# Low parts of the retention weights: accumulating transfers in place of VectorE subtractions, and an earlier latent statistic

## The chip, the cores and the metric

One core of one Trainium2 chip runs the whole program. The metric is the device time of one execution in microseconds (us). The kernel before was timed three times: 1770.57, 1771.42 and 1773.42 us, median 1771.42 us.

## What is computed

Two layers of a diffusion backbone work on 512 latent tokens and 256 context tokens of width 1024. Layer 0 is windowed attention with a SwiGLU feed-forward part; layer 1 is bidirectional retention with a second SwiGLU. The change lies where layer 0 hands over to layer 1 and in layer 1's retention, cut here to what matters:

```python
def bidir_retention(h_x, h_c, w_qkvg, decay_logit, gn_gain, w_o, need_ctx_out):
    q_x, k_x, v_x, g_x = jnp.split(h_x @ w_qkvg, [qk, 2 * qk, 2 * qk + RET_VWIDTH], axis=-1)
    ...
    k_c, v_c = jnp.split(h_c @ w_qkvg[:, qk:2 * qk + RET_VWIDTH], [qk], axis=-1)
    ...
    ox_f, _ = retention_chunked(q_x, k_x, v_x, log_g[0], state_f)
    ox_b, _ = retention_chunked(flip(q_x), flip(k_x), flip(v_x), log_g[1], state_b)
    out_x = gated_out(ox_f + flip(ox_b), g_x)

# around it, for each layer
h_x = modulate(rms_norm(x, norm1_g[i]), mx[0], mx[1])
h_c = modulate(rms_norm(y_ctx, norm1_g[i]), mc[0], mc[1])
```

There are 4 retention heads, each with 256 query and key columns and 512 value and gate columns. All is float32.

## The kernel before

**Two parts of every operand.** The TensorE (PE) works on a rounded float32 type. So each float32 operand is split into a high part (the rounded value) and a low part (the operand minus the high part), and each product is three matmuls: high x high, low x high, high x low (`mm3`, `product_q`, `product_v`). The second of them already needs the weight's low part.

**A weight on its way.** Weights lie in DRAM as a row of chunks `wst[i]`, 128 x 1024 each (512 KB). `chunk(i)` (line 1155) starts the load on SP's queue into a raw buffer: `wraw`, of which there are 2, or `wx`, of which there are 4 and which the retention's scores use too. `w_parts` (line 126) hands out one of four pairs of buffers `whi`, `wlo`, two in the pool `rp` and two in `qp`, in turn. `split` (line 164) writes `whi` by a cast on ACT and `wlo` by a subtraction on VectorE (DVE). `split_chunk` (line 1160) does this for q, k, v and g weights and keeps its last instruction in `last_split`, on which some orders of instructions are hung; `next_w` (line 136) loads, casts and subtracts in one for the output weights. A pair of buffers is free again when PE has done its last product with it, a raw buffer when its last reader is done.

**The products are of Strassen's kind.** The tokens and the rows of the weights are cut in halves, and one of the weight operands is a sum or difference of chunks, made by DVE in place in the raw buffers. For the query and key of a head (lines 1352 to 1358), q12 = q22 - q12 (L1353), k11 = q12 + k11 (L1354), w2 is the split of this k11, k21 = k21 - k11 (L1356), k11 = q22 - k11 (L1357), and w1, w3, w22, w4 are the splits of k11, q12, q22, k21. For gate and value it is L1388, L1389 and L1394 (w2, w3, w4), and after the scores L1454 (w1).

**The order in a head** (loop at line 1310): key weights k11, k21 and their products with latent and context tokens; the five query products w2, w1, w3, w22, w4; rotation of the query; the second half of the value weights, b21 (in head 0 this comes before the keys); w2, w3, w4 of gate and value; six rounds of scores and outputs (lines 1414 to 1448); w1 and w22 of the gate; norm and gate; the first value weights of the next head (`first_weights_v`); the output projection (`out_tile`), 2 tiles per weight chunk. In the last head the output is done in two halves, between them the first weights of the next feed-forward part (`first_weights`, line 1546), which keep their own cast and subtraction.

**Queues.** SP issues the raw loads in order. In this part nobody uses POOL's queue, but for some adds of squares in the last head. Each engine works in order; the order on each engine is set by a scheduler when the program is built, except in stretches marked as written by hand, which are not touched here.

**The hand-over.** `output(prev, True)` (line 1132) makes the last output tiles of layer 0: 8 latent tiles, then 8 context tiles. `square_and_stats` (line 1035) is called after each. For a latent tile it adds its square into a running sum (ACT and DVE). For a context tile it squares it on ACT and adds it up over partitions with a matmul by ones into a PSUM bank of the pair `pj`; after the second context tile it switches ACT's table (`ln_exp_turn`) and makes the latent statistic (`rms(0)`), whose bank is the other one of the pair.

Of the kernel before, what the change touches and what calls it, by code (L numbers as in the profile page):

```python
# [11 lines left out]
AF = mybir.ActivationFunctionType  # L12
# [4 lines left out]
KT = D // P  # L17
SX = 512
SC = 256
# [30 lines left out]
def dit_kernel(ctx, tc, xT, cT, crow, small, consts, masks, tabs0, tabs1, jtab, adaQ, adaN, adaT, wst, out):  # L50
    nc = tc.nc
    mult, add, sub = ALU.mult, ALU.add, ALU.subtract
# [9 lines left out]
    def T(pool, cols, tag, bufs, dt=F32):  # L62
        return pool.tile([P, cols], dt, tag=tag, bufs=bufs, name=tag)

    def pj(n=512):
        return T(psJ, 512, "pj", 2)[:, :n]
# [6 lines left out]
    ones = cp.tile([P, P], F32, name="ones_sb")  # L73
# [17 lines left out]
    def after(ins, others):  # L91
        for o in others:
            tc.add_manual_dep(ins.ins, o.ins.name, order, reason="table set turn")

    def ln_exp_turn():
        pre = nc.scalar.preload_act_table_set("natural_log_exp_and_others")
        after(pre, turn["silu"])
        turn.update(pre=pre, lnexp=[], silu=[])
# [19 lines left out]
    wpos, wsel, ring = [0], [0], []  # L118

    def w_raw(pool=None, bufs=2):  # L120
        raw = T(pool or rp, 1024, "wraw", bufs)
        nc.sync.dma_start(raw, wst[wpos[0]])
        wpos[0] += 1
        return raw

    def w_parts(pool, own=2):

        bufs = own
        if ring:
            pool, bufs = ring[wsel[0] % len(ring)], 2  # L130
        elif wsel[0] % (2 + own) < 2:
            pool, bufs = rp, 2
        wsel[0] += 1
        return T(pool, 1024, "whi", bufs, F32R), T(pool, 1024, "wlo", bufs, F32R)

    def next_w(pool, own=2, raw=None):

        raw = raw or w_raw()
        hi, lo = w_parts(pool, own)
        nc.scalar.copy(hi, raw)  # L140
        nc.vector.tensor_tensor(lo, raw, hi, op=sub)  # L141
        return hi, lo

    def mm3(o, w, x, first, last):

# [18 lines left out]
    def split(t, hi, lo):  # L164
        nc.scalar.copy(hi, t)  # L165
        return nc.vector.tensor_tensor(lo, t, hi, op=sub)  # L166


    def load_stream(s, engines=(nc.sync, nc.sync)):
        res = []  # L170
        if s == 0:
            for k in range(KT):
                t = T(rp, 512, "res", 12)
                eng = engines[k % 2] if k < 4 else nc.sync
                ins = eng.dma_start(t, xT[:, k, :])
                if eng is nc.scalar:
                    turn["lnexp"].append(ins)
                res.append(t)
        else:
            for k in range(0, KT, 2):  # L180
                t = T(rp, 512, "res", 12)
                nc.sync.dma_start(t.rearrange("p (a n) -> p a n", a=2), cT[:, k:k + 2, :])
                res += [t[:, 0:SC], t[:, SC:2 * SC]]
        return res

    def t_sq(n):
        return T(rp, 512, "sq", 2)[:, :n]
# [7 lines left out]
    def neg_half_rstd(y, z, tot, count, behind=()):  # L195

        after(lnexp(y, tot, AF.Ln, scale=1.0 / count, bias=eps), behind)
        lnexp(y, y, AF.Exp, scale=-0.5)
        nc.scalar.activation(z, y, AF.Square, scale=0.5 / math.sqrt(count))
        nc.vector.scalar_tensor_tensor(z, tot, count * EPS, z, add, mult)  # L200
        nc.vector.scalar_tensor_tensor(y, z, -0.75, y, add, mult)
# [3 lines left out]
    def add_square(s, k, t, c=slice(None), eng=nc.vector, tmp=t_sq, fresh=True):  # L205

        if k == 0:
            if fresh:
                ssq[s] = t_y(s)
            return nc.scalar.activation(ssq[s][:, c], t[:, c], AF.Square)  # L210
        sq = tmp(NTOK[s])[:, c]
        ins = nc.scalar.activation(sq, t[:, c], AF.Square)
        eng.tensor_tensor(ssq[s][:, c], ssq[s][:, c], sq, op=add)
        return ins

    def rms(s, c=slice(None), bank=pj, behind=()):
        y = ssq[s][:, c]
        n = y.shape[1]
        tot = bank()[:, :n]
        after(nc.tensor.matmul(tot, ones, y, start=True, stop=True), behind)  # L220
        neg_half_rstd(y, t_sq(n), tot, D)
# [150 lines left out]
    raw = []  # L372
# [444 lines left out]
    for g in range(NKV):  # L817
        final = g == NKV - 1
        for i, (s, b) in enumerate(context + latent if final else latent + context):
# [7 lines left out]
            if final and i > 1:  # L827
                d = early[i - 2]
# [3 lines left out]
        if g == 2:  # L832
            split_o(2)
            wo0 = wpos[0]
            cres = load_stream(1)
# [11 lines left out]
    for d4 in range(0, KT, 4):  # L847
        wpos[0] = wo0 + max(d4, 2)
        w = [next_w(wo_p) if d > 1 else wo_w[d] for d in range(d4, d4 + 4)]
# [183 lines left out]
    ctx_sum = []  # L1033

    def square_and_stats(s, d, t):
        if s == 0:
            add_square(s, d, t)
            return
        if d == 0:
            ctx_sum.append(pj(SC))  # L1040
        sq = t_sq(SC)
        nc.scalar.activation(sq, t, AF.Square)
        nc.tensor.matmul(ctx_sum[0], ones, sq, start=d == 0, stop=d == KT - 1, skip_group_check=True)
        if d == 1:
            ln_exp_turn()
            rms(0)

    def spare_w():

        raw, w = w_raw(), (T(fp, 1024, "wraw", 1, F32R), T(fp, 1024, "adaw", 1, F32R))  # L1050
        split(raw, *w)
        return w
# [95 lines left out]
    qp = R.enter_context(tc.tile_pool(name="qp", bufs=1, reuse_waits="tile"))  # L1148
# [4 lines left out]
    chunk_base = wpos[0]  # L1153

    def chunk(i, own=False):
        raw = T(qw, 1024, "wx", 4) if own else T(rp, 1024, "wraw", 2)
        nc.sync.dma_start(raw, wst[i])
        return raw

    def split_chunk(raw):  # L1160
        w = w_parts(qp)
        last_split[0] = split(raw, *w)
        return w

    last_split, hm = [None], []

# [67 lines left out]
    def product_v(os, a, w, first, tiles=(0, 1), by_k=False):  # L1234

        for t, k in ((t, k) for k in range(4) for t in tiles) if by_k else ((t, k) for t in tiles for k in range(4)):
            tok = slice(t * P, t * P + P)
            whi, wlo = (p[:, k % 2 * 512:k % 2 * 512 + 512] for p in w[k // 2])
            xhi, xlo = (x[:, tok] for x in a(k))
            for i, (p, r) in enumerate(((xhi, whi), (xhi, wlo), (xlo, whi))):  # L1240
                ins = nc.tensor.matmul(os[t], p, r, start=first and k + i == 0, stop=k == 3 and i == 2,  # L1241
                                       skip_group_check=by_k or not first)
        return ins
# [42 lines left out]
        return t[:, 0:512], t[:, 512:1024]  # L1286

    def first_weights_v(hd):
        return [split_chunk(chunk(chunk_base + 16 * hd + 4 + i)) for i in range(2)]

    def values_first(w, by_k=False):

# [17 lines left out]
    for hd in range(RH):  # L1310
        bq = chunk_base + 16 * hd
        bv, bg = bq + 4, bq + 8

        def other_values():

            b21 = [split_chunk(chunk(bv + i)) for i in (2, 3)]
            Xv = [W4("X"), W4("X")]
            product_v(Xv, quarter_of("12"), b21, True)
            for t in range(2):
                nc.vector.tensor_tensor(vt[t], vt[t], Xv[t], op=add)  # L1320
            c = cv if hd else context_values(b11)
            product_v(c, context_half(1), b21, False)
            vt.extend((T(rp, 512, "y0", 1), T(qp, 512, "vc", 1)))
            for t in range(2):
                nc.scalar.copy(vt[4 + t], c[t])

        if hd == 0:
            other_values()
        k11, k21 = split_chunk(chunk(bq)), split_chunk(chunk(bq + 1))
        if hd == 0:  # L1330
            sums = token_sums(hm, 0, T(qp, 64, "sh2", 1), h_sum, [normed])
            dx, dcx = strips(0, [sums])
# [19 lines left out]
        q12, q22, k11, k21 = chunk(bq + 2, True), chunk(bq + 3, True), chunk(bq), chunk(bq + 1)  # L1352
# [2 lines left out]
        w2 = split_chunk(k11)  # L1355
        nc.vector.tensor_tensor(k21, k21, k11, op=sub)  # L1356
        nc.vector.tensor_tensor(k11, q22, k11, op=sub)  # L1357
        w1, w3, w22, w4 = (split_chunk(r) for r in (k11, q12, q22, k21))
        while strip_sums:
            after(strip_sums.pop(), [last_split[0]])  # L1360
        Y2 = W4("Y")
# [20 lines left out]
        g12, w2, w4 = [], [], []  # L1382
# [8 lines left out]
        w3 = [split_chunk(g) for g in g12]  # L1391
# [59 lines left out]
        w1 = []  # L1451
        for i in range(2):
            g, v = chunk(bg + i), chunk(bv + i)
            nc.vector.tensor_tensor(g, g, v, op=sub)  # L1454
            w1.append(split_chunk(g))
        w22 = [split_chunk(chunk(bg + 2 + i)) for i in range(2)]
        Zg = [W4("Z"), W4("Z")]
        last = hd == RH - 1
        product_v(Zg, quarter_of(1), w1, True)
# [10 lines left out]
        r, z = mv[:, 8:12], mv[:, 12:16]  # L1470
# [53 lines left out]
        w = []  # L1524

        def out_tile(d, c, tags="XY"):
            while len(w) * 2 <= d:
                w.append(next_w(qp))
            oo = (W4(tags[d % 2]) if tags[d % 2] != "j" else pj())[:, c]
            for k in range(4):  # L1530
                c0 = k * 256 + (d % 2) * P
                mm3(oo, (w[d // 2][0][:, c0:c0 + P], w[d // 2][1][:, c0:c0 + P]),
                    (yt[k][0][:, c], yt[k][1][:, c]), k == 0, k == 3)
            return nc.vector.scalar_tensor_tensor(xr[d][:, c], oo, mods[1, 0][:, 2, d:d + 1], xr[d][:, c], mult, add)

        if hd < RH - 1:
            for d in range(KT):
                out_tile(d, slice(0, SX))
            continue
        w += [next_w(qp) for _ in range(4)]  # L1540
        H.close()
        hM, hW, hX = (ctx.enter_context(tc.tile_pool(name=n, bufs=1, reuse_waits="tile", side="right"))
                      for n in ("hM", "hW", "hX"))
# [141 lines left out]
    for gsz in FFN_GROUPS:  # L1685
        acts = []
        for i in range(gsz):
            if f < 2:
                acts.append(first[f])
            elif f == 2:  # L1690
                w = [next_w(fp), next_w(fp)]
# [153 lines left out]
```

## Time and profile before

| | before |
|---|---|
| median of three runs | 1771.42 us |
| the profiled execution | 1769.85 us |
| its span in the trace | 1768.1 us |
| PE clock granted | 1.00 (mean 0.999) |
| DMA engines' busy share in the retention part (890 to 1415 us) | 0.40 |
| splits of a weight chunk there | 100 (25 per head) |

"Busy" is the time in which an engine had an instruction of the program at work. PE's matmuls overlap and their ends are modelled, so PE's busy time is an upper bound. A row of groups gives line, engine, operation, output and inputs with their shapes, the count, and after the bar the busy time in us, the mean of one in ns, and the idle time before them with what ended it. A row of a timeline gives start and length in us. `PEld` is PE's weight load, `SPq` an issue on SP's queue.

### The profile page before, as it was taken

How to read it: one execution, taken by the hardware profiler on the slowest of the kernel's cores; microseconds unless marked ns; L12 is line 12 of the kernel's file. 1: busy time of each engine (PE TensorE's matmuls, PEld its weight loads, DVE VectorE, ACT ScalarE, POOL GpSimd, SP SyncE). 2: the span in 40 equal slices, each digit the busy share in tenths (PEclk: the TensorE clock that was granted, in tenths of full speed). 3: DMA queues.
4: the chain of work that ended last, by engine and by line, in shares of the span. 5: the costliest groups of instructions: out<-in, count | busy, mean ns of one | idle time of the engine just before them, and what ended most of it. 6: DMA issues, size and time to landing. Idle time of an engine off the chain costs nothing.

```text
span 1768.1 us, 27617 instructions
## 1 busy us (share of the span) xinstructions
PE 1720.8 (97%) x10876; PEld 1526.5 (86%) x10876; DVE 1355.5 (77%) x2368; ACT 843.8 (48%) x1480; POOL 131.1 (7%) x268
## 2 busy tenths in 40 slices
PE   8999999999999999999998999999999999999999
PEld 5777777789999899999987788898897889999998
DVE  6697778788779787777789858758768897777774
ACT  5576676464433334342465534534524564445442
POOL 0034434000000000000000000000000000000000
PEclk9999999999999999999999999999999999999999
DMA  9501012533243534343343534434433323233322
GB/s 352 224 15 35 25 49 72 180 114 136 74 142 119 167 119 144 121 141 116 99 133 107 161 98 138 155 96 134 153 99 116 96 86 113 90 108 108 96 84 84
DMA packets 60754, 207.73 MB, mean 117 GB/s; under 512 B 6736, under 2 KB 7120, under 8 KB 60368
## 3 DMA queue, kind: packets, MB, share of 16 engines
q1 hardware_dynamic: 53424, 180.28, 31.6%
q0 software_dynamic: 6912, 25.17, 4.6%
q8 instruction: 85, 1.39, 0.3%
q10 hardware_dynamic: 288, 0.52, 0.1%
q14 instruction: 45, 0.37, 0.1%
HBM read 203.85 MB, written 2.10 MB: 116 GB/s over the span
## 4 chain that ended last, share of the span: by engine, by line
PE 66%; DVE 17%; DMA 9%; ACT 3%; issue 3%; POOL 1%; SPq 0%; ACTq 0%; DVEq 0%; POOLq 0%
PE Y L874 13%; PE Z L874 6%; PE pj L150 6%; PE pj L149 6%; PE pj L148 6%; DMA wraw<-in_wst_dram 4%; PE X L874 3%; DVE wlo L166 3%; PE Z L1241 3%; PE Y L1230 3%; PE pT L725 2%; DMA adaw<-in_adaT_dram 2%; DVE y L274 2%; PE pO L737 2%; PE pj L1241 1%
## 5 line engine op out<-in xcount | busy, mean ns | idle before, releaser
L165 ACT CAST whi<-wraw 128x1024 fp32r<-128x1024 f32 x177 | 185.4, 1051 | 294.7 <-PE Z L150 65.3
L166 DVE TENSOR_TENSOR wlo<-wraw,whi 128x1024 fp32r<-128x1024 f32 x177 | 215.9, 1222 | 41.8 <-ACT whi L165 41.7
L874 PE MATMUL Y<-aq,whi 128*128 128x384 f32 x640 | 173.8, 335 | 0.8 <-ACT hn L1014 0.5
L256 DVE SCALAR_TENSOR_TENSOR res<-pj,mod,res 128x512 f32<-128x512 f32 (+1 forms) x112 | 81.6, 729 | 57.0 <-PE pj L150 56.4
L141 DVE TENSOR_TENSOR wlo<-wraw,whi 128x1024 fp32r<-128x1024 f32 x81 | 99.7, 1230 | 30.9 <-ACT whi L140 30.1
L874 PEld LDWEIGHTS Y<-aq,whi 128*128 128x128 f32 x640 | 116.5, 188 | 2.4 <-ACT hn L1014 1.1
L140 ACT CAST whi<-wraw 128x1024 fp32r<-128x1024 f32 x81 | 84.9, 1050 | 70.4 <-PE Z L150 22.2
L874 PE MATMUL Y<-aq,wlo 128*128 128x384 f32 x320 | 107.2, 335 | 1.9 <-DVE wlo L166 1.9
L101 ACT ACTIVATE pr<-pr,stat,qs 128x513 f32<-128x513 f32 (+2 forms) x96 | 74.3, 776 | 17.9 <-DVE stat L709 17.8
L1241 PE MATMUL Z<-whi,sA 128*128 128x512 f32 x256 | 81.0, 392 | 1.8 <-ACT whi L165 1.8
L716 POOL TENSOR_SCALAR pr<-pr,stat 128x512 f32<-128x512 f32 (+2 forms) x96 | 71.8, 761 | 77.8 <-DVE stat L713 54.2
L274 DVE CUSTOM_DVE_ANT_0 y<-adaw,crow,small_sb 128x1024 bf16<-128x1024 f32 x48 | 61.4, 1280 | 16.2 <-DMA adaw<-in_adaT_dram 16.2
L148 PE MATMUL pj<-ax,whi 128*128 128x512 f32 x176 | 68.7, 391 | 1.0 <-DVE res L256 1.0
L150 PE MATMUL pj<-ax,whi 128*128 128x512 f32 x176 | 68.6, 390 | 0.0
L149 PE MATMUL pj<-ax,wlo 128*128 128x512 f32 x176 | 68.5, 389 | 0.0
L148 PE MATMUL pj<-act,whi 128*128 128x512 f32 x168 | 66.0, 393 | 0.0
L149 PE MATMUL pj<-act,wlo 128*128 128x512 f32 x168 | 65.9, 392 | 0.0
L150 PE MATMUL pj<-act,whi 128*128 128x512 f32 x168 | 65.5, 390 | 0.0
L725 PE MATMUL pT<-const_sb,pr 128*128 128x128 f32 x352 | 57.0, 283 | 8.5 <-POOL pr L716 5.1
L874 PEld LDWEIGHTS Y<-aq,wlo 128*128 128x128 f32 x320 | 60.1, 188 | 2.5 <-DVE wlo L166 2.5
L725 PEld LDWEIGHTS pT<-const_sb,pr 128*128 128x128 f32 x352 | 38.4, 141 | 26.5 <-POOL pr L716 15.3
L874 PE MATMUL Y<-sA,whi 128*128 128x256 f32 x304 | 60.8, 283 | 0.2 <-ACT res L1647 0.2
(549 smaller groups left out, 5246.2 us busy)
## 6 DMA issues: line engine op xcount, KB each, us to landing
wraw<-in_wst_dram SPq DMA_DIRECT2D x240, 512.0 KB, 3.6
adaw<-in_adaT_dram POOLq DMA_DIRECT2D x32, 512.0 KB, 3.9
wx<-in_wst_dram SPq DMA_DIRECT2D x24, 512.0 KB, 4.8
adan<-in_adaQ_dram SPq DMA_DIRECT2D x16, 512.0 KB, 8.2
crow<-in_adaT_dram POOLq DMA_DIRECT2D x16, 512.0 KB, 4.3
adan<-in_adaN_dram SPq DMA_DIRECT2D x12, 512.0 KB, 7.6
adaw<-in_adaT_dram SPq DMA_DIRECT2D x8, 512.0 KB, 4.3
res<-in_xT_dram SPq DMA_DIRECT2D x14, 256.0 KB, 3.8
```

The costliest lines, as they stand in the source:

```text
L140: nc.scalar.copy(hi, raw)
L141: nc.vector.tensor_tensor(lo, raw, hi, op=sub)
L148: nc.tensor.matmul(o, whi, xhi, start=first, stop=False)
L149: nc.tensor.matmul(o, wlo, xhi, start=False, stop=False)
L150: return nc.tensor.matmul(o, whi, xlo, start=False, stop=last)
L165: nc.scalar.copy(hi, t)
L166: return nc.vector.tensor_tensor(lo, t, hi, op=sub)
L256: return nc.vector.scalar_tensor_tensor(res[d], o, mods[l, s][:, part, d:d + 1], res[d], mult, add)
L274: after(nc.vector.tensor_tensor_reduce(junk, w, cr[:, s * 1024:(s + 1) * 1024], 1.0, sm_t[:, C_ADAB + l * 48 + j:C_ADAB + l * 48 + j + 1], ...
L725: nc.tensor.transpose(tp[:, a * P:(a + 1) * P], self.pr[(0, 2, 1, 3)[a]][:, ki * P:(ki + 1) * P], ident)
L874: nc.tensor.matmul(o, p, r, start=first and k + i == 0, stop=k == 3 and i == 2, skip_group_check=not first)
L1241: ins = nc.tensor.matmul(os[t], p, r, start=first and k + i == 0, stop=k == 3 and i == 2, skip_group_check=by_k or not first)
```

## The change

A new function `split_dma` makes the low part without DVE: ACT writes the high part, then ACT writes minus the high part into the low part's buffer, then a transfer issued on POOL's queue adds the operand into it. The operand is read from the raw buffer, or from DRAM a second time where the chunk is used as it was loaded (`whole_chunk`), which leaves the raw buffer to its next load after the cast. All `split_chunk` calls and the retention's output weights (`next_w` with `by_dma=True`) take this way; 13 of a head's 25 read DRAM, 12 the raw buffer. `split` stays for the activations, for the other layers' weights, and for the first weights of the next feed-forward part.

In `square_and_stats`, the bank of the context's sum is now taken after `rms(0)`, and the square of a context tile follows two tiles later, the last three after the last tile.

```diff
-    def next_w(pool, own=2, raw=None):
+    def next_w(pool, own=2, raw=None, by_dma=False):
 
         raw = raw or w_raw()
-        hi, lo = w_parts(pool, own)
-        nc.scalar.copy(hi, raw)
-        nc.vector.tensor_tensor(lo, raw, hi, op=sub)
-        return hi, lo
+        w = w_parts(pool, own)
+        if by_dma:
+            split_dma(raw, *w, wst[wpos[0] - 1])
+        else:
+            split(raw, *w)
+        return w
...
+    def split_dma(t, hi, lo, src=None):
+
+        nc.scalar.copy(hi, t)
+        nc.scalar.activation(lo, hi, AF.Identity, scale=-1.0)
+        return nc.gpsimd.dma_start(lo, t if src is None else src, accum_op=add)
...
-        if d == 0:
-            ctx_sum.append(pj(SC))
-        sq = t_sq(SC)
-        nc.scalar.activation(sq, t, AF.Square)
-        nc.tensor.matmul(ctx_sum[0], ones, sq, start=d == 0, stop=d == KT - 1, skip_group_check=True)
         if d == 1:
             ln_exp_turn()
             rms(0)
+            ctx_sum.append(pj(SC))
+        for k in ((d - 2,) if 1 < d < KT - 1 else range(KT - 3, KT) if d == KT - 1 else ()):
+            sq = t_sq(SC)
+            nc.scalar.activation(sq, cres[k], AF.Square)
+            nc.tensor.matmul(ctx_sum[0], ones, sq, start=k == 0, stop=k == KT - 1, skip_group_check=True)
...
-    def split_chunk(raw):
+    def split_chunk(raw, i=None):
         w = w_parts(qp)
-        last_split[0] = split(raw, *w)
+        last_split[0] = split_dma(raw, *w, None if i is None else wst[i])
         return w
+
+    def whole_chunk(i):
+        return split_chunk(chunk(i), i)
...
-        return [split_chunk(chunk(chunk_base + 16 * hd + 4 + i)) for i in range(2)]
+        return [whole_chunk(chunk_base + 16 * hd + 4 + i) for i in range(2)]
...
-            b21 = [split_chunk(chunk(bv + i)) for i in (2, 3)]
+            b21 = [whole_chunk(bv + i) for i in (2, 3)]
...
-        k11, k21 = split_chunk(chunk(bq)), split_chunk(chunk(bq + 1))
+        k11, k21 = whole_chunk(bq), whole_chunk(bq + 1)
...
-        w1, w3, w22, w4 = (split_chunk(r) for r in (k11, q12, q22, k21))
+        w1, w3, w22, w4 = (split_chunk(r, i) for r, i in ((k11, None), (q12, None), (q22, bq + 3), (k21, None)))
...
-        w22 = [split_chunk(chunk(bg + 2 + i)) for i in range(2)]
+        w22 = [whole_chunk(bg + 2 + i) for i in range(2)]
...
-                w.append(next_w(qp))
+                w.append(next_w(qp, by_dma=True))
...
-        w += [next_w(qp) for _ in range(4)]
+        w += [next_w(qp, by_dma=True) for _ in range(4)]
```

## The prediction

> **What bounds the kernel now.** I read the page first, then the busy times by stretch, then the timelines of the stretches that lose time.
>
> ```profile
> span 1768.1 us, 27617 instructions
> ...
> PE 1720.8 (97%) x10876; PEld 1526.5 (86%) x10876; DVE 1355.5 (77%) x2368; ACT 843.8 (48%) x1480; POOL 131.1 (7%) x268
> ```
>
> TensorE (PE) is busy for 97% of the span, so no edit to another engine can give back more than PE's idle time. The change touches only the retention part, from 890 to 1415 us. In the busy times by stretch the columns are PE, PE's weight loads, DVE, ACT, POOL, PE's clock, DMA share and GB/s:
>
> ```profile
> 890.00:1415.00 525.00, 512.32 (x2791) 440.33 (x2790) 402.79 (x582) 247.44 (x385) 4.04 (x8) 1.00 0.40 125
> ...
> 930.00:940.00 10.00, 8.33 (x67) 7.93 (x66) 10.00 (x19) 5.98 (x10) 0.00 (x0) 1.00 0.16 54
> 940.00:950.00 10.00, 9.06 (x76) 8.86 (x75) 8.16 (x10) 4.13 (x8) 0.00 (x0) 1.00 0.59 203
> 950.00:960.00 10.00, 8.22 (x57) 7.26 (x55) 10.00 (x16) 5.70 (x8) 0.00 (x0) 1.00 0.39 114
> 960.00:970.00 10.00, 8.29 (x36) 6.30 (x34) 10.00 (x12) 4.10 (x6) 0.00 (x0) 1.00 0.12 34
> 970.00:980.00 10.00, 9.27 (x40) 7.45 (x41) 8.17 (x13) 5.64 (x9) 0.00 (x0) 1.00 0.74 231
> 980.00:990.00 10.00, 9.43 (x41) 7.18 (x40) 7.54 (x10) 5.32 (x7) 0.00 (x0) 1.00 0.40 116
> ```
>
> Of 525 us PE is idle for 525 - 512.32 = 12.7 us, the ceiling of any gain. The six stretches of head 0 from 930 to 990 hold 1.67 + 0.94 + 1.78 + 1.71 + 0.73 + 0.57 = 7.4 us of it, and there DVE is full (10.00 in three of them). So VectorE bounds the first head in places, and PE bounds the other three heads.
>
> **The part that goes: the subtractions.** The groups of instructions between 890 and 1415 us:
>
> ```profile
> L166 DVE TENSOR_TENSOR wlo<-wraw,whi 128x1024 fp32r<-128x1024 f32 x60 | 73.2, 1222 | 24.5 <-ACT whi L165 24.5
> L165 ACT CAST whi<-wraw 128x1024 fp32r<-128x1024 f32 x60 | 62.9, 1049 | 93.1 <-PE Y L150 52.6 <-DMA wraw<-in_wst_dram 16.0 <-DVE wraw L1454 15.0
> L166 DVE TENSOR_TENSOR wlo<-wx,whi 128x1024 fp32r<-128x1024 f32 x24 | 28.8, 1222 | 11.3 <-ACT whi L165 11.1
> L141 DVE TENSOR_TENSOR wlo<-wraw,whi 128x1024 fp32r<-128x1024 f32 x16 | 19.6, 1225 | 14.6 <-ACT whi L140 14.1
> ```
>
> All 60 + 24 + 16 = 100 go, 25 a head: 121.6 us of DVE's 402.79. In heads 1 to 3 this is worth almost nothing by itself, since PE is the bound. In head 0 I credit the whole idle time of the six rows: **-7.4 us** (bounds 0 and -7.4).
>
> **The part that comes on ACT and POOL.** 100 negations of 128x1024 on ACT, priced by the cast of the same shape at 1.05 us: 105 us, so ACT goes from 247 to 352 of 525 us. It stays under PE, but it is in order, so a negation can stand in front of a PSUM copy. POOL has 4.04 us of work in the stretch; its queue is free for 100 issues, each waiting for its negation, with nothing else behind it but the next issue and, in the last head, POOL's adds of squares. I add **+1.1 us** for one negation in front of one copy at the tail, where nothing covers it (bounds 0, and 4 x 1.05 = 4.2 for the last head's four output weights).
>
> **How late a low part becomes.** An accumulating transfer is not in this trace. The nearest rows are plain loads of the same 512 KB; the last two numbers are KB and us from issue to landing:
>
> ```profile
> wraw<-in_wst_dram SPq DMA_DIRECT2D x240, 512.0 KB, 3.6
> adaw<-in_adaT_dram POOLq DMA_DIRECT2D x32, 512.0 KB, 3.9
> adan<-in_adaQ_dram SPq DMA_DIRECT2D x16, 512.0 KB, 8.2
> ...
> q1 hardware_dynamic: 53424, 180.28, 31.6%
> ```
>
> The least is 3.9 us (POOL's own queue); the most that I allow is 8.2 us, the slowest median of a 512 KB load. The engines' time of one pass is 31.6% of 1768.1 us over 180.28 MB, which is 1.62 us for 0.524 MB. An accumulating transfer must also read what it adds to, so I take 3.9 + 1.6 = **5.5 us**. A low part then lands 1.05 + 5.5 = 6.55 us after its high part instead of 1.22 us: 5.3 us later, 100 times. Where the weight is made far ahead of its use this is hidden:
>
> ```profile
> 1031.32 1.06 ACT L165 CAST whi<-wraw 128x1024 fp32r<-128x1024 f32 x1 [4.34 <-PE Y L150]
> ...
> 1047.60 2.87 PE Y L1230 x24
> ```
>
> The first row is the cast of head 1's k11, the second (the chain) its first product, 16 us later; I price k and the output weights at nothing. The cover is those 16 us, less 7.6 for cast, negation and transfer. It is not hidden where a weight is made just in time.
>
> **Head 0, query weights.** Timeline of DVE and ACT (start, length):
>
> ```profile
> 903.14 1.22 DVE L166 TENSOR_TENSOR wlo<-wraw,whi 128x1024 fp32r<-128x1024 f32 x1
> ...
> 920.60 2.35 DVE L166 TENSOR_TENSOR wlo<-wraw,whi 128x1024 fp32r<-128x1024 f32 x2
> ...
> 935.17 1.22 DVE L1354 TENSOR_TENSOR wraw<-wx,wraw 128x1024 f32<-128x1024 f32 x1
> 938.05 1.22 DVE L166 TENSOR_TENSOR wlo<-wraw,whi 128x1024 fp32r<-128x1024 f32 x1
> 939.52 1.22 DVE L1357 TENSOR_TENSOR wraw<-wx,wraw 128x1024 f32<-128x1024 f32 x1
> ...
> 936.42 1.05 ACT L165 CAST whi<-wraw 128x1024 fp32r<-128x1024 f32 x1 [0.39 <-DVE wraw L1354]
> ```
>
> PE got w2's high part at 937.5 and stood until its low part was done at 939.3. Five subtractions ahead of L1354 go (the first and the last two are shown), so it can start some 5.5 us sooner, near 929.7. Then: sum done 930.9, cast and negation 933.0, transfer landed 938.5. Against 937.5, w2 costs 1.0 us. w1 is worse: L1357 overwrites k11, which w2's transfer still reads. It waits until 938.5, ends 939.7, cast and negation 941.8, landed 947.3. PE finishes w2 at 938.5 + 2.87 = 941.4 (one chunk's 24 products take 2.87 us in the chain), so w1 costs 5.9 us. The four products left end at 947.3 + 4 x 2.87 = 958.8.
>
> Next late are head 0's value weights, whose raw buffer is held until w1's transfer has read it. SP's queue, then DVE:
>
> ```profile
> 943.36 0.33 SPq L1157 DMA_DIRECT2D wraw<-in_wst_dram  x1
> ...
> 948.21 1.23 DVE L1388 TENSOR_TENSOR wx<-wraw,wx 128x1024 f32<-128x1024 f32 x1 [1.81 <-DMA wraw<-in_wst_dram]
> 949.47 1.23 DVE L1389 TENSOR_TENSOR wx<-wx 128x1024 f32<-128x1024 f32 x1
> ```
>
> The load that left at 943.36 leaves 3.9 us later, and so does L1388, at 952.1. Two sums, cast, negation and transfer end at 952.1 + 2.5 + 2.1 + 5.5 = 962.2, against 958.9: 3.3 us. Head 0 pays 1.0 + 5.9 + 3.3 = **+10.2 us** (the same steps with a transfer of 3.9 us: 0 + 3.7 + 1.8 = 5.5; with 8.2 us: 3.7 + 8.6 + 6.1 = 18.4).
>
> **Heads 1 to 3, value weights.** Chain row, then DVE and ACT of head 1:
>
> ```profile
> 1078.98 5.45 PE pj L1241 x24
> ...
> 1069.13 1.23 DVE L166 TENSOR_TENSOR wlo<-wraw,whi 128x1024 fp32r<-128x1024 f32 x1 [0.58 <-ACT whi L165]
> ...
> 1079.68 1.23 DVE L166 TENSOR_TENSOR wlo<-wx,whi 128x1024 fp32r<-128x1024 f32 x1
> ...
> 1083.09 1.22 DVE L1389 TENSOR_TENSOR wx<-wx 128x1024 f32<-128x1024 f32 x1
> ...
> 1084.94 2.94 ACT L165 CAST whi<-wx 128x1024 fp32r<-128x1024 f32 x3
> ```
>
> PE starts the value product at 1084.4 and needs the second chunk's low part 13 matmuls of 0.227 us (5.45 / 24) later, near 1087.2. The second sum (L1389) ends 1084.3; without the two subtractions ahead of it, 1081.9. Cast and negation 1084.1, landed 1089.6: 2.4 us late, three heads: **+7.2 us** (at 3.9 us 2.4; at 8.2 us 15.3). The third operand's chunks are cast when the context product frees their buffers at 1084.4; the first lands at 1084.4 + 2.1 + 5.5 = 1092.0, when PE, with the 2.4 us, reaches it at 1084.4 + 5.45 + 2.4 = 1092.2. I price them at nothing: their cover is that earlier wait, and without it they are 2.2 us late a head.
>
> **The squares.** PE's waits, and the sums over partitions of the context:
>
> ```profile
> PEld pj L1043 <- ACT sq L1042: 1.3, 5, 0.5
> ...
> L1043 PE MATMUL pj<-sq,ones_sb x16: 378/379/484, 888.1 to 903.4; 128*128 128x256 f32 x16
> ```
>
> The same eight ACT squares and 16 matmuls stay; they run two tiles later, so PE need not wait for them, and the latent statistic goes ahead. **-1.3 us**; the upper bound is +1.1, three squares' products gathered at the end (6 x 0.38 = 2.3 us) half uncovered. The context norm does not wait for that: it stands behind the first value product.
>
> **Sum.** -7.4 + 1.1 + 10.2 + 7.2 - 1.3 = +9.8 us on the profiled execution's 1769.85 us (span 1768.1 and 1.75 around it): 1779.7 us. The median shown, 1771.42, is 0.09% above that execution; I forecast by the execution. With 3.9 us a transfer the sum is -7.4 + 1.1 + 5.5 + 2.4 - 1.3 = +0.3; with 8.2 us, -7.4 + 1.1 + 18.4 + 15.3 - 1.3 = +26.1. The forecast's own range is 1773 to 1796.
>
> **Rivals.** *A, faster: the order absorbs the transfers.* The waits above keep today's order of products. w3, w22 and w4 do not depend on w1; three products are 8.6 us, more than w1's 5.9, and the weights' sums can be put earlier on a DVE that has lost 30% of its work. Then -7.4 - 1.3 = -8.7 stays: 1761. For it: PE already runs products in an order fitted to readiness, as w2's, where 12 matmuls of the first chunk run before the second is touched. Against it: k11's overwrite and the held raw buffers cannot be reordered away, and only four pairs of weight buffers exist. It decides if a transfer lands within about 4 us.
>
> *B, much slower: the 16 DMA engines become the bound.*
>
> ```profile
> 1060.00:1100.00 40.00, 39.69 (x228) 34.52 (x227) 33.19 (x41) 18.65 (x29) 0.00 (x0) 1.00 0.43 132
> ```
>
> In these 40 us the engines are busy 0.43 x 40 = 17 us. Ten weights are cast in them; if each transfer takes two passes, 10 x 2 x 1.62 = 32 us come on top, 50 in 40: +9.6 us a head, four heads +38: 1808. At one pass it is 33 of 40, no bound. For it speaks that the data moved doubles; against it, that the stretch from 1100 to 1130 and the output products have room. The Trainium skill (Collectives: The Full Stack, "The bandwidth ceiling: the fold count and why AG ≠ RS ≠ AR") says that an add in a transfer costs two reads on one ring and so halves its rate; by that the engines' time would be these two passes and the sum would be rival B. No row here shows it.
>
> *C, no change.* The transfer costs no more than POOL's plain load, 3.9 us: sum +0.3, 1770.2. The queue's row speaks for it, the extra read against it.
>
> **How the numbers follow.** The forecast has 0.42, A 0.34, B 0.14, C 0.10. Predicted: 1779.7 us. The range 1759 to 1804 leaves out the lower half of A's spread below 1759 and most of B. About 0.2% is what a measurement of this kernel can tell from no change. Faster 0.34 (A), same 0.10 (C), slower 0.56 (forecast and B).
>
> **What would show it.** In the changed profile: no subtraction into wlo on DVE between 890 and 1400 (the next layer's first weights keep theirs); DVE near 281 us and ACT near 352 there; 100 more POOL issues, with their landing (5.5 us; 3.9 and 8.2 are the bounds). PE's longest waits in head 0 should name a transfer into wlo, after the first query product, 4 to 8 us; in heads 1 to 3 one of 1 to 5 us a head at the first value product. A landing under 4 us, or PE waits on wlo under 3 us in sum, makes the forecast wrong towards A; a DMA share over 0.9 from 1060 to 1100 makes it wrong towards B.

## The result and the profile after

The changed kernel takes 1896.8 us (median of 4 runs, 1895.92 to 1902.62), the kernel before beside it 1770.99 us (4 runs, 1770.52 to 1773.42): ratio 1.0715, interval 1.0701 to 1.0729, so 126 us slower. The direction was forecast, the size was not: 1779.7 us was predicted, and 1804 was the end of the range.

From the page of the changed kernel the span, the engines' busy time and POOL's DMA queue (packets, MB, share of 16 engines' span), then POOL's queue on the page before:

```profile
span 1895.5 us, 27904 instructions
...
PE 1761.5 (93%) x10876; PEld 1548.5 (82%) x10876; DVE 1242.0 (66%) x2268; ACT 939.4 (50%) x1580; POOL 218.6 (12%) x368
...
q0 software_dynamic: 21312, 77.60, 19.4%
```

```profile
q0 software_dynamic: 6912, 25.17, 4.6%
```

The work moved as the diff says: DVE has 100 instructions fewer, ACT and POOL 100 more, and POOL's queue carries 52.4 MB more. That took 19.4% of 1895.5 less 4.6% of 1768.1, which is 367.7 - 81.3 = 286 us of the 16 engines, 2.86 us a transfer; one plain pass was reckoned at 1.62. For the same 10876 products PE is busy 40.7 us longer than before (1761.5 for 1720.8), and its granted clock is 0.975 in the mean for 0.999; the other 87 us of the longer span are PE standing. Since the ends of products are modelled, this division is rough.

Where the time went is read from PE's first product of an output tile, in head 0 and in head 3. The timeline before (start, length), then after:

```profile
1025.68 0.39 PE L148 MATMUL X<-qk,whi 128*128 128x512 f32 x1
...
1403.37 0.28 PE L148 MATMUL X<-qk,whi 128*128 128x256 f32 x1
```

```profile
1054.83 0.39 PE L150 MATMUL X<-qk,whi 128*128 128x512 f32 x1
...
1531.73 0.28 PE L150 MATMUL X<-qk,whi 128*128 128x256 f32 x1
```

Head 0 is 29.2 us late by then, head 3 128.4: so heads 1 to 3 lose 33 us each in the mean, no less than head 0, where VectorE was full before. The busy times by stretch after, in the prediction's columns (the last two are DMA share and GB/s):

```profile
890.00:1415.00 525.00, 451.18 (x2257) 377.10 (x2255) 225.32 (x369) 280.32 (x389) 74.27 (x85) 0.93 0.75 186
...
1030.00:1040.00 10.00, 8.23 (x37) 6.01 (x35) 6.50 (x10) 6.13 (x8) 1.74 (x2) 1.00 1.04 350
1040.00:1050.00 10.00, 8.52 (x35) 6.66 (x36) 1.02 (x2) 5.97 (x8) 1.74 (x2) 0.83 1.06 262
1060.00:1100.00 40.00, 37.02 (x243) 33.93 (x242) 10.83 (x16) 18.85 (x24) 7.01 (x8) 1.00 0.77 178
```

PE now stands for 525 - 451.18 = 74 us of this stretch (12.7 before), and its granted clock is 0.93 there. The DMA share is 0.75 for 0.40, and for 20 us in a row it is 1.04 and more (the share adds up the times of the packets, and where packets overlap it can pass 1). VectorE and ACT are far from full. What PE waits for directly (us in total, times, the longest), from 890 to 1545 us:

```profile
PE X L1252 <- DMA wlo<-in_wst_dram: 20.8, 4, 8.8
PE Z L1252 <- DMA wlo<-wx: 17.9, 10, 3.1
PE Z L1252 <- DMA wlo<-in_wst_dram: 10.4, 5, 3.8
```

In all, 68 of the 99 us that PE waits directly are for transfers into low parts. The DMA issues of the same stretch (KB, median us to landing), after and then before:

```profile
wraw<-in_wst_dram SPq DMA_DIRECT2D x91, 512.0 KB, 5.0
wlo<-in_wst_dram POOLq DMA_DIRECT2D x52, 512.0 KB, 8.2
wlo<-wraw POOLq DMA_DIRECT2D x28, 512.0 KB, 5.1
wx<-in_wst_dram SPq DMA_DIRECT2D x24, 512.0 KB, 9.0
wlo<-wx POOLq DMA_DIRECT2D x20, 512.0 KB, 6.3
```

```profile
wx<-in_wst_dram SPq DMA_DIRECT2D x24, 512.0 KB, 4.8
```

The transfers land in 5.1 to 8.2 us, and the plain loads beside them are late too: 9.0 us into `wx` for 4.8, 5.0 into `wraw` for 3.6. PE's longest wait shows how the two chain. SP, ACT, POOL and PE of the changed kernel, then the landing of the load in the first row and the busy times while it was under way:

```profile
1412.21 0.33 SPq L1165 DMA_DIRECT2D wraw<-in_wst_dram  x1
1423.09 1.05 ACT L172 CAST whi<-wraw 128x1024 fp32r<-128x1024 f32 x1 [9.81 <-DMA wraw<-in_wst_dram]
1425.53 0.88 POOL L174 DMA_DIRECT2D wlo<-in_wst_dram  x1 [11.08 <-ACT wlo L173]
1434.12 0.80 PE L1252 MATMUL X<-wlo,aq 128*128 128x512 f32 x1 [8.79 <-DMA wlo<-in_wst_dram]
...
wraw<-in_wst_dram SPq DMA_DIRECT2D x1, 512.0 KB, 10.8
...
1412.00:1423.00 11.00, 8.78 (x69) 8.06 (x67) 4.51 (x9) 1.25 (x2) 0.88 (x1) 1.00 1.02 265
```

The plain load issued at 1412.21 lands after 10.8 us, three times the median of 3.6 before; three transfers, issued at 1407.68, 1410.28 and 1413.57, are in part under way beside it, and the DMA share is 1.02. Its chunk is cast at 1423.09 and negated, and its own transfer, issued at 1425.53, lands at 1434.0. So one late load and one transfer make 21.9 us from the load's issue to PE's product, of which PE could not cover 8.8. A held raw buffer is near by, but not on this path: SP's next load, at 1419.42, waited 6.9 us for the transfer of 1410.28, which was still reading its buffer.

### The profile page after: what moved, and what is told of

The parts are those of the page before. It is cut to its first block, busy times and chain, and to the rows that moved or that the text cites. A ratio compares the mean times of both kernels' runs of the same rounds, so it can differ in the third digit from the quotient of the medians.

```text
span 1895.5 us, 27904 instructions
## 1 busy us (share of the span) xinstructions
PE 1761.5 (93%) x10876; PEld 1548.5 (82%) x10876; DVE 1242.0 (66%) x2268; ACT 939.4 (50%) x1580; POOL 218.6 (12%) x368
## 3 DMA queue, kind: packets, MB, share of 16 engines
q0 software_dynamic: 21312, 77.60, 19.4%
## 4 chain that ended last, share of the span: by engine, by line
PE 59%; DMA 16%; DVE 12%; issue 6%; ACT 4%; POOL 2%; SPq 0%; DVEq 0%; POOLq 0%; ACTq 0%
PE Y L882 11%; PE Z L882 5%; PE pj L151 5%; PE pj L150 5%; PE pj L152 5%; DMA wraw<-in_wst_dram 5%; DMA wlo<-in_wst_dram 4%; PE Z L1252 4%; PE X L882 3%; PE X L1241 2%; PE pT L733 2%; DMA wlo<-wx 2%; PE Y L1241 2%; DMA adaw<-in_adaT_dram 2%; DVE y L282 2%
## 5 line engine op out<-in xcount | busy, mean ns | idle before, releaser
L168 DVE TENSOR_TENSOR wlo<-wraw,whi 128x1024 fp32r<-128x1024 f32 x182 | 222.8, 1226 | 33.3 <-ACT whi L167 32.7
L173 ACT ACTIVATE wlo<-whi 128x1024 fp32r<-128x1024 f32 x100 | 104.8, 1056 | 1.2
L1252 PE MATMUL Z<-whi,sA 128*128 128x512 f32 x256 | 88.7, 420 | 7.8 <-DVE gate L1472 7.8
L174 POOL DMA_DIRECT2D wlo<-in_wst_dram x52 | 45.5, 876 | 304.6 <-ACT wlo L173 202.3
L1252 PE MATMUL Z<-wlo,sA 128*128 128x512 f32 x128 | 54.8, 428 | 17.9 <-DMA wlo<-wx 17.9
L1252 PEld LDWEIGHTS Z<-whi,sA 128*128 128x128 f32 x256 | 52.5, 205 | 20.1 <-DVE gate L1472 8.6
```

The costliest lines, as they stand in the source:

```text
L173: nc.scalar.activation(lo, hi, AF.Identity, scale=-1.0)
```

## The experiments

Theory 1 was that each low part comes late and holds its raw buffer (a matter of latency), Theory 2 that the 16 engines are the bound (a matter of load). Times are medians, and the differences are against the kernel before in the same batch. e2 to e13 all contain the change's edit of the squares too, so that a difference of -2.5 us, as e1 has it, is inside each of them.

| kernel | us | ratio (interval) | against before |
|---|---|---|---|
| e1 squares alone | 1770.72 | 0.9990 (0.9981 to 0.9999) | -2.5 |
| e2 output weights | 1789.21 | 1.0086 (1.0066 to 1.0106) | +16.0 |
| e3 chunks read from DRAM | 1827.55 | 1.0304 (1.0290 to 1.0318) | +54.4 |
| e4 chunks read from SBUF | 1830.80 | 1.0324 (1.0306 to 1.0343) | +57.6 |
| e5 negations, no transfer | 1790.38 | 1.0108 (1.0093 to 1.0123) | +18.4 |
| e6 transfers of an eighth | 1802.47 | 1.0169 (1.0152 to 1.0186) | +30.5 |
| e7 load beside | 1860.58 | 1.0506 (1.0490 to 1.0522) | +88.6 |
| e8 plain copies | 1824.90 | 1.0305 (1.0290 to 1.0321) | +52.9 |
| e9 half the load beside | 1801.72 | 1.0173 (1.0160 to 1.0187) | +31.0 |
| e10 all read from the raw buffer | 1928.51 | 1.0877 (1.0861 to 1.0894) | +157.8 |
| e11 k weights alone | 1772.65 | 1.0012 (1.0003 to 1.0021) | +1.9 |
| e12 negations and load beside | 1867.61 | 1.0540 (1.0522 to 1.0559) | +95.7 |
| e13 load that holds nothing | 1848.59 | 1.0441 (1.0424 to 1.0458) | +77.9 |

**One part of the change at a time: e1 to e4.** e1 takes the squares' edit onto the kernel before; e2 adds the transfers of the 16 output weights; e3 the 52 chunks that the transfer reads from DRAM (those 16 among them); e4 has only the 48 sums that it reads from SBUF.

```diff
 (e2: every split_chunk by VectorE)
-        last_split[0] = split_dma(raw, *w, None if i is None else wst[i])
+        last_split[0] = split(raw, *w)
```

> Only the later squares and the earlier latent statistic, no transfers. If the 126 us all come from the transfers: 1769 to 1772 us, within 0.2% of before. If the moved squares take part: more than 3 us above before.

> Transfers for the 16 output weights only (squares as in the change). Theory 1 (the low part comes late and raw buffers are held; a transfer made far ahead of its use costs nothing): 0 to +3 us. Theory 2 (the 16 DMA engines are the bound, so every transfer costs the same 126 / 100 = 1.26 us): +20 us.

> Transfers for the 52 chunks that are used as loaded and read a second time from DRAM; the 48 sums keep their subtraction. In the changed profile PE waits 45.5 us directly for such transfers. Theory 1: +45 to +65 us. Theory 2: 52 x 1.26 = +66 us.

> Transfers for the 48 sums only, read from the raw buffers; the chunks used as loaded keep their subtraction. PE waits 22.6 us directly for such transfers in the changed profile. Theory 1: +20 to +40 us. Theory 2: 48 x 1.26 = +60 us.

e1 is at the edge of what can be told from no change: the kernel before took 1773.18 us in its batch, and 1770.67 to 1772.00 in the others. Against e1, e3 costs 56.8 us and e4 60.1, so the parts make -2.5 + 56.8 + 60.1 = 114.4 of 126 us, and there is no one bad place. By the differences a transfer costs 1.0 us in e2, 1.05 in e3 and 1.2 in e4. e2 and e4 lie near Theory 2's 20 and 60 us and above Theory 1's ranges; e3's 54.4 lies inside Theory 1's range and 12 us under Theory 2's 66. So the nearly equal prices spoke for Theory 2, but not clearly. And e2's trace shows a wait, not a full engine. ACT, POOL and PE of e2, then VectorE and PE of the kernel before for the same first chunk of the output:

```profile
1016.46 1.05 ACT L172 CAST whi<-wraw 128x1024 fp32r<-128x1024 f32 x1
...
1019.52 1.07 ACT L173 ACTIVATE wlo<-whi 128x1024 fp32r<-128x1024 f32 x1
...
1020.89 0.90 POOL L174 DMA_DIRECT2D wlo<-in_wst_dram  x1 [166.03 <-ACT wlo L173]
...
1029.03 0.60 PE L151 MATMUL X<-qk,wlo 128*128 128x512 f32 x1 [3.61 <-DMA wlo<-in_wst_dram]
```

```profile
1018.20 1.23 DVE L141 TENSOR_TENSOR wlo<-wraw,whi 128x1024 fp32r<-128x1024 f32 x1 [1.81 <-ACT whi L140]
...
1025.90 0.39 PE L149 MATMUL X<-qk,wlo 128*128 128x512 f32 x1
```

From the cast to the landed low part it is 1029.0 - 1016.5 = 12.6 us: the next cast and other work stand in front of the negation for 2 us, and issue and landing take 8.1. VectorE had the low part at 1019.4, and PE asked for it 6.5 us later. Nearly equal prices came about by different means.

**ACT alone, and few bytes: e5 and e6.** In e5 VectorE makes the low part over the negation; in e6 the transfer carries 128 of 1024 columns.

```diff
 (e5)
-        return nc.gpsimd.dma_start(lo, t if src is None else src, accum_op=add)
+        return nc.vector.tensor_tensor(lo, t, hi, op=sub)
 (e6)
-        nc.scalar.activation(lo, hi, AF.Identity, scale=-1.0)
-        return nc.gpsimd.dma_start(lo, t if src is None else src, accum_op=add)
+        nc.scalar.activation(lo[:, 896:], hi[:, 896:], AF.Identity, scale=-1.0)
+        nc.vector.tensor_tensor(lo[:, :896], t[:, :896], hi[:, :896], op=sub)
+        src = t if src is None else src
+        return nc.gpsimd.dma_start(lo[:, 896:], src[:, 896:], accum_op=add)
```

> The changed kernel with its 100 negations on ACT, but the low parts then made by VectorE's subtraction over them (no transfer). It prices ACT's part alone, about 126 us being the whole loss. Theory 1 (the low part comes late, by the time of the transfer): a low part is late by one negation, 1.05 us of some 8.5, so +2 to +12 us, 1773 to 1783. Theory 2 (the 16 DMA engines are the bound): no transfer, no loss, 1769 to 1773. A third theory (negations stand in front of ACT's copies and casts): +30 us or more, 1800 and above.

> The changed kernel, but each transfer carries only the last 128 of 1024 columns (64 KB for 512 KB); ACT negates these columns, VectorE subtracts the other 896. The transfers' number, their place in the queue and their holding of the raw buffers stay, their bytes fall to an eighth. Theory 1 (lateness: issue 0.87 us and the fixed part of the landing, about 4 us, stay): a low part is still late by 5 of 8 us, so at least half of the 126 us stays, 1835 to 1880. Theory 2 (engines): 2.86 us of 16 engines a transfer fall to under 0.6 (small rows), loss under 25 us, 1771 to 1796.

e5 costs 18.4 us, more than Theory 1 said and less than the third: PE's longest waits in it (us in total, times, the longest) are for the low part that now comes a negation later.

```profile
PE Z L1252 <- DVE wlo L174: 9.9, 8, 2.9
```

e6 lies far below Theory 1's 1835 and just above Theory 2's 1796. Two rows of its landings in the stretch:

```profile
wlo<-in_wst_dram POOLq DMA_DIRECT2D x52, 64.0 KB, 4.6
wlo<-wraw POOLq DMA_DIRECT2D x28, 64.0 KB, 2.6
```

With all 100 issues in place and every raw buffer still read by a transfer, an eighth of the bytes leaves a quarter of the loss. So issue and whatever of the landing does not depend on the bytes are not the main part. But e6 shortens the landings as well (4.6 for 8.2 us, 2.6 for 5.1) and takes seven eighths of each negation from ACT, so by itself it does not tell the load from the lateness.

**The load without the wait: e7, e9, e12, e13.** VectorE makes all low parts. 100 transfers go into a scratch in DRAM beside it. Of each edit only the added lines are shown.

```diff
 (e7, without the negation; e9 the same with hi[:, :512] and spare[n][:, :512]; e12 keeps the negation)
+        beside.append(nc.gpsimd.dma_start(spare[n], hi.bitcast(F32), accum_op=add, max_dma_last_dim=4096))
+        return nc.vector.tensor_tensor(lo, t, hi, op=sub)
 (e13, without the negation)
+        mark = nc.gpsimd.tensor_copy(T(qp, 2, "mark", 2)[:, 0:1], hi[:, 0:1].bitcast(F32))
+        beside.append(nc.gpsimd.dma_start(spare[n], wst[n], accum_op=add, max_dma_last_dim=4096))
+        after(beside[-1], [mark])
+        return nc.vector.tensor_tensor(lo, t, hi, op=sub)
```

> VectorE makes all low parts as before; beside it 100 accumulating transfers of 512 KB of the high part into a scratch in DRAM that nobody reads, issued by POOL when the high part is there. The DMA engines and POOL's queue are loaded as in the changed kernel, but no low part waits for a transfer and no raw buffer is held; there is no negation. Theory 1 (lateness and held buffers): under +15 us, 1771 to 1786. Theory 2 (engines): the raw loads and tables come late as in the changed kernel, +80 us or more, 1850 and above.

> As the load beside the kernel (100 accumulating transfers of the high part into a scratch in DRAM, low parts by VectorE, +89 us), but of 512 columns in place of 1024: the same number of transfers, half of the bytes. If the engines' time is what counts, the loss falls at least in proportion: 45 us if each byte costs alike (1817), under 25 us if the loss comes only where the engines run full (under 1797; the mean share falls from 0.83 to about 0.62). If the number of transfers counts (issue, queue), most of the 89 us stays, 1840 and above.

> The load beside the kernel (100 accumulating transfers into a scratch, low parts by VectorE, +89 us) and the 100 negations on ACT (alone +18 us) in one kernel: all work that the change adds on ACT, POOL and the DMA engines, but no low part waits for a transfer and no raw buffer is held by one. VectorE keeps its subtractions. If the two prices add up: +107 us, 1873 to 1883, and what is left to the changed kernel's 126, some 19 us, is the price of waiting for the transfers and of held buffers. If both load the same slack: +85 to +95, 1856 to 1866. If they make each other worse, 1890 or more, and waiting for the transfers then costs nothing beyond the load.

> The load beside the kernel once more, but each transfer adds a chunk of DRAM to the scratch in DRAM instead of reading the high part: a copy of one column of the high part on POOL sets when it goes, and no buffer of the kernel waits for its landing (in the first load the high part's buffer was held for 7.4 us). Same number and bytes. If the engines' load is the price: +75 to +100, 1847 to 1872. If the first load's +89 came from held buffers: under +30, 1802 or less.

e7's +88.6 fits Theory 2, but its transfers hold the high parts' buffers. e13 takes that away and still costs 77.9 us. Its queue, its busy times by stretch, the landing of its plain loads, PE's waits and ACT's:

```profile
q0 software_dynamic: 21312, 77.60, 19.7%
...
890.00:1390.00 500.00, 456.62 (x2365) 389.33 (x2363) 334.73 (x473) 203.84 (x312) 143.82 (x174) 0.95 0.82 204
...
wraw<-in_wst_dram SPq DMA_DIRECT2D x100, 512.0 KB, 5.2
...
PE pj L1443 <- DVE qk L168: 14.9, 4, 4.9
PE Z L1257 <- ACT whi L174: 10.9, 4, 3.1
...
ACT whi L174 <- DMA wraw<-in_wst_dram: 84.5, 31, 7.2
```

ACT's casts of a chunk before, for the last row:

```profile
ACT whi L165 <- DMA wraw<-in_wst_dram: 16.0, 13, 2.0
```

Its engines' time is (0.197 x 1847.2 - 81.3) / 100 = 2.83 us a transfer, the changed kernel's 2.86. No instruction of the kernel waits for one of these transfers; the chunks come late, ACT waits 84.5 us for them instead of 16.0, and PE waits for ACT and VectorE. VectorE and ACT do their own work no slower: they are busy for 1354.5 us and 843.3 (1355.5 and 843.8 before). So the load alone makes 78 us, on DMA engines that are busy for 0.82 of the stretch in the mean. e9 tells how steep that is. Its queue and stretch, then e7's queue:

```profile
q0 software_dynamic: 21312, 51.39, 15.1%
...
890.00:1390.00 500.00, 468.96 (x2471) 397.43 (x2470) 359.84 (x501) 219.81 (x334) 82.13 (x95) 0.99 0.70 170
```

```profile
q0 software_dynamic: 21312, 77.60, 20.9%
```

Half the bytes cost 35% of the loss, between its two bounds for a price by load (25 and 45 us) and far from a price by count; per transfer the engines were busy for 1.91 us ((0.151 x 1801.2 - 81.3) / 100) and 3.07. So the first 62% of the load's time, up to a share of 0.70, makes 35% of the loss, and the rest is dearer. It also bounds what 100 issues by POOL can cost apart from the bytes: 31 us. e12 adds the negations to e7 and costs 7 us more, not 18, just above the range for a shared slack (up to +95) and far below the sum (+107): for the most part the two use the same slack. What the changed kernel loses beyond e12 is 30 us; that is about the price of waiting for the transfers and of held raw buffers, not cleanly, since e12 keeps VectorE's subtractions and its transfers hold the high parts. No run parts the two.

**The change with cheaper transfers, and with longer holding: e8, e10.**

```diff
 (e8)
+        return nc.gpsimd.dma_start(lo, t if src is None else src)
 (e10)
+        return nc.gpsimd.dma_start(lo, t, accum_op=add)
```

> The changed kernel with its transfers as plain copies of the chunk over the negated high part, without the accumulation (the low part is then the chunk itself): the same number, queue, waits and held buffers, but one pass of the engines for 1.76. Theory 1 (lateness): the landing falls from 7.4 to about 5 us, so of 8.5 us of delay about 6 stay, loss 70 to 100 us, 1840 to 1870. Theory 2 (engines): their share falls by 124 us in all, from 0.77 to about 0.53 in the retention part, no bound: loss under 40 us, 1771 to 1811.

> The changed kernel with all 100 transfers reading the chunk from its raw buffer in SBUF; the 52 second reads of DRAM go, and 52 more raw buffers are held until their transfer has landed. Engines' time (the bytes that the engines move are the same): within 20 us of the changed kernel, 1877 to 1917. If the second read of DRAM is the costly part (those transfers landed in 8.2 us, the others in 5.1 and 6.3): 30 us or more faster, 1867 or less. If held raw buffers are the costly part: over 1917.

```profile
q0 software_dynamic: 21312, 77.60, 13.3%
```

e8 leaves out the addition, so that its low parts are the chunks themselves. A plain copy takes (0.133 x 1823.0 - 81.3) / 100 = 1.61 us of the engines. With every issue and every negation in place, taking 1.25 us of engine time from each transfer gives back 126 - 53 = 73 us, near e13's 78. But the landings are shorter too (5.1 us from DRAM for 8.2), so these 73 are load and lateness together. The 52.9 lie between the two theories' ranges; if prices add, 18 of them are e5's negations, though e12 showed that they need not. e10 shows what holding costs: 52 reads of DRAM fewer, and yet 32 us slower than the change. That was the third outcome. Its transfers take no more of the engines, (0.186 x 1933.1 - 81.3) / 100 = 2.78 us each, but 52 more raw buffers wait for a landing, and the next loads with them. ACT's waits for loaded chunks, in e10 and then in the changed kernel:

```profile
ACT whi L172 <- DMA wraw<-in_wst_dram: 133.1, 33, 10.1
```

```profile
ACT whi L172 <- DMA wraw<-in_wst_dram: 35.3, 11, 10.1
```

e10's and e4's transfers touch no DRAM and e13's touch no SBUF, and all three kernels lose 58 us or more: so far as this goes, the price does not hang on one of the two memories. What they share is the 16 engines and POOL's queue.

**k alone: e11.** The first two weights of each head by transfer, all others by VectorE, and the squares.

> The squares' edit and only the first two weights of each head (k) by transfer, 8 of 100; all others by VectorE. The prediction priced them at nothing, for 16 us between cast and product; and VectorE, which is full in head 0, loses 2.4 us there. By the cover of 16 us: 1766 to 1772, faster if head 0's time on VectorE comes back. By an equal price of about 1.2 us a transfer (the four parts run so far): +8 to +10 us, 1778 to 1782.

```profile
wlo<-in_wst_dram POOLq DMA_DIRECT2D x8, 512.0 KB, 6.4
...
PE Y L1241 <- DMA wlo<-in_wst_dram: 3.4, 1, 3.4
```

1772.65 us is just outside the range by cover and far from the 1778 of an equal price. +1.9 us for 8 transfers are 0.24 each, or 0.55 if the squares alone are worth -2.5 in it: where the lead is long and the engines have room, a transfer costs little, even at a landing of 6.4 us. The one wait for one, 3.4 us, is in head 0, where k's lead is short. The relief of VectorE in head 0 did not show as a gain.

## Why the prediction was wrong

**The failed step** is the pricing of a transfer as a fixed delay of 5.5 us ("How late a low part becomes"), which beyond its own low part touches only k11's overwrite and one raw buffer of head 0, with the engines' load set apart as rival B and a price only past a share of 1. Apart from that one buffer, the plain loads were left at their old times. e13 shows what that left out: 78 us at a mean share of 0.82, through plain loads that come late. Rival B had the right resource, with two passes of 1.62 us for measured 1.76 passes, and forecast +38. From 1060 to 1100 us, where it had 50 us of work for 40, the share was 0.77; the same work came some 29 us later by then, and from 1089 to 1129 it was 0.76. The work did not stay above one; it came in bursts, such as the 20 us from 1030 and those from 1089 to 1109 (0.99), and the loads behind a burst were late, as the one of 10.8 us. The Trainium skill (Collectives: The Full Stack, "The bandwidth ceiling: the fold count and why AG ≠ RS ≠ AR") says that an add reads twice and so halves the rate of its ring; 2.86 us against 1.61 for the same plain copy is 1.78, so the runs here nearly agree.

**The transfer's time.** The landing, 5.1 to 8.2 us, was inside the bounds of 3.9 and 8.2, and even the sum made with 8.2 gave only +26.1. So a better landing would not have saved the forecast. A slip in the working weighs little: 13 products of 0.227 us behind 1084.4 end at 1087.4, not 1087.2, which makes 2.2 us a head for 2.4.

**ACT.** 100 negations of 1.06 us were priced rightly one by one, but at +1.1 us in sum, with cover everywhere but at the tail; alone (e5, squares included) they cost 18.4. A term mis-sized: in every head the negation stands between the cast and the low part, and in front of other work of ACT.

**Head 0.** L1354's sum did start early, as forecast, at 929.08 for 929.7 (L1365 after). VectorE's rows of head 0, then its wait in all heads:

```profile
929.08 1.22 DVE L1365 TENSOR_TENSOR wraw<-wx,wraw 128x1024 f32<-128x1024 f32 x1
...
944.09 1.23 DVE L1368 TENSOR_TENSOR wraw<-wx,wraw 128x1024 f32<-128x1024 f32 x1
...
DVE wraw L1368 <- DMA wlo<-wraw: 4.6, 3, 2.8
```

The overwrite of k11 began at 944.1, where 938.5 was forecast, but there VectorE came to it from other work without standing; the three of the later heads did wait for w2's transfer, 4.6 us in sum. So the mechanism exists and is small on VectorE. Of 2.8 us net for head 0 (10.2 less 7.4), 29.2 came by its output products.

**Heads 1 to 3** got 2.4 us each, for one late value weight; 33 came. This is the largest miss, and it follows from the failed step: only a weight made just in time was counted, and with the loads late more of them are such; PE's waits above name several kinds, the longest that of 8.8 us behind a plain load that took 10.8. How the 33 us divide between late loads, the transfers' landing, ACT and held buffers is known only as far as e5, e10, e12 and e13 go.

**k and the output weights.** For k the cover of 16 us held but for one wait in head 0 (e11). For the output weights the same row was used without looking at theirs, where 7.7 us lay between VectorE's start and PE's product; alone (e2, squares included) they cost 16.0 us.

**The squares.** The waits went as forecast: of the 1.3 us that PE's weight loads waited for squares, this is left in e1:

```profile
PEld pj L1046 <- ACT sq L1045: 0.2, 1, 0.2
```

That the time falls with them is not shown: e1's -2.5 us stand against the slowest batch of the kernel before, and its interval reaches 0.9999.

**Rivals A and C** fell. The order absorbed nothing beyond k. The check set for B, a share over 0.9 from 1060 to 1100, read 0.77 though the engines' load was the main price: a mean over 40 us does not show the bursts.

## What to carry to other kernels

Work moved from an engine with slack to the DMA engines must be priced against the loads that they already carry, over stretches as short as a load's lead: at a share of 0.4 another 0.4 is not free, since loads that feed the pipeline come late long before the mean reaches 1. An operation replaced by a transfer also becomes a longer hold on its source buffer (e10); ask which load waits for that buffer. And a cover read from one weight's row belongs to that weight only.

## What the runs showed of the hardware

An accumulating transfer of 512 KB took 2.86 us of the 16 engines in the changed kernel, 2.83 in e13 and 3.07 in e7; a plain copy in the same queue took 1.61, and an accumulating one of half the size into DRAM 1.91, more than half of e7's 3.07. With only 16 of them (e2) it was (0.073 x 1786.6 - 81.3) / 16 = 3.07 too, so this price is no product of the crowding. POOL spent 0.87 us on each issue.

The clock adds to a long wait. PE of the changed kernel behind the wait of 8.8 us, and that stretch by its granted clock:

```profile
1434.71 1.06 PE L1252 MATMUL X<-whi,aq 128*128 128x512 f32 x2
1435.56 0.63 PE L1252 MATMUL X<-wlo,aq 128*128 128x512 f32 x1
...
1438.41 0.62 PE L1252 MATMUL X<-whi,aq 128*128 128x512 f32 x2
1438.86 0.40 PE L1252 MATMUL X<-wlo,aq 128*128 128x512 f32 x1
...
1430.00:1440.00 10.00, 5.88 (x18) 4.73 (x19) 2.90 (x4) 1.46 (x2) 0.00 (x0) 0.61 0.26 60
```

Two products start 0.85 us ahead of the third at first, 0.425 us each; some 4 us behind the wait's end two take 0.45, 0.225 each. The Trainium skill (TensorE: Matmul & The Clock Gate, "What's actually happening") says that the array falls to half its clock after an idle window of about 3.4 us and needs as long a busy one to come back; this stretch agrees. So the wait of 8.8 us costs PE some 1.5 us more behind it, by this estimate: the ten products that start from 1434.71 on take 3.7 us, until 1438.41, and would take 2.25 at 0.225 each.
